# First head of a hybrid streaming step: epsilon rows by a small matmul, queries evacuated sooner, the fourth weight split later on VectorE, values stored ahead of keys

## Chip, cores and metric

One core of a Trainium2 chip runs the whole program in one launch. The metric is the device time in microseconds (us); the median of several executions is compared. Engines are named as the profile does: PE is TensorE, PEld its weight loads, DVE VectorE, ACT ScalarE, POOL GpSimd, SP the queue that issues nearly all DMAs.

## The reference

One layer of an encoder, on 512 frames of a new stream and 64 frames of a running one with 512 cached keys and values. Cut to what matters here:

```python
hn = rmsnorm(x, g_norm1)                       # x / sqrt(mean(x^2) + EPS) * g
proj = hn @ w_in                               # 2048 -> q, k, v (8 heads x 128), gb, gc, hc
q = rmsnorm(q.reshape(B, T, N_HEADS, HEAD_DIM), g_q)
k = rmsnorm(k.reshape(B, T, N_HEADS, HEAD_DIM), g_k)
o_attn = stick_breaking_blocks(q, k_all, v_all, P)   # strictly causal, cached and new keys
...                                            # gated short convolution, output norms
x = x + mix @ w_out
h2 = rmsnorm(x, g_norm2)
x = x + (silu(h2 @ w_gate) * (h2 @ w_up)) @ w_down
# outputs: y, and the new k, v and convolution state of both streams
```

## The kernel before

All 576 tokens (512 + 64) lie along the free axis in two halves of 288, the features on 128 partitions. Every product is made of three passes in a rounded f32 form: each operand is split into a high part (a cast on ScalarE) and a low part (a subtraction, L178 for weights, L225 elsewhere), and TensorE adds high x high, low x high, high x low (`step`, L215). A projection of 128 columns is 2 halves x 16 steps x 3 matmuls. The input norm's row scale isn't applied to x: the projections of q and k use it only through the epsilon of their own norm (EPS times the row's mean square, `eps_r`, 18 columns of 128), and values are multiplied by a broadcast row scale `R1`.

Weights go through a chain: `load_weight` starts a DMA into one of two raw buffers, `split_weight` makes the halves, `next_weight` hands them out in the order q, k, v of head 0, q, k, v of head 1 and so on. So weight 3, the fourth, is the query weight of head 1.

Work other than projections is written as generators on a `Pipeline`. It counts one tick after each step of a projection, 32 to a projection; a generator yields the number of ticks after which it goes on. In head 0 the keys' projection has the ticks 1 to 32, the values' 33 to 64, and head 1's queries begin at 65. The order of TensorE's instructions is this written order throughout, and from head 1 on SP's too. The order of VectorE, ScalarE and GpSimd in the heads (and of SP in head 0) is set by a planner at build time, which simulates all engines and prefers what was written earlier. Each engine then runs its own list strictly in order.

For head 0 the query product is already formed while the input is turned. Then come, as written: the five diagonals `dg` of the row scale, the split of weight 2, and `q_evac` (a 32x32 transpose of the product into `E`, L661, squares L662, sums L663). Behind the keys' projection, `row_scale` makes R1 with five small matmuls (L460), turns it on VectorE (L464) and takes a reciprocal of the square for `eps_r` (L466 to L468). The rest of a norm (`rest`) adds the column sums with one small matmul (ss, L639), makes the reciprocal root (ms L643, y L644 and L645 on ScalarE, t L646 and L647, r L648), scales E (L649), turns it back (qf or kf, L653) and splits it (qh and ql, kh and kl); it runs 38 ticks after the queries' end and 8 after the keys'. For the keys it also makes `kb`, the form that is stored (GpSimd, L651), and starts `attend`.

`attend` begins 24 ticks later in head 0 with the scores z (L708, z0 to z2) and the scores of the cached keys (zs, L734), 10 ticks later stores kb with eight DMAs (L678), after 18 more goes on with the weights (L751 and following) and after 26 more makes the output product po (L772, L775), which needs `vh` and `vl`, the halves of the values. `values` turns the values (L813), stores them to scratch memory 8 ticks after its start, reloads them as `vtok` 12 later (L818, L819), and 8 later stores them to the output (L821, L822) and splits them. `x_sums` forms sums of the input for a later product, in steps between all this. The turned cached keys `kcT` (L831) are made 59 ticks after head 0's start; the buffer of cached keys can be refilled after that.

Of the kernel before, what the change touches and what calls it, by code (L numbers as in the profile page):

```python
# [31 lines left out]
EPS = 1e-6  # L32
# [62 lines left out]
def tile_hybrid_stream_step(  # L95
# [6 lines left out]
    nc = tc.nc  # L102
    mm = nc.tensor.matmul
# [17 lines left out]
    rpad = ctx.enter_context(tc.tile_pool(name="rpad", bufs=1, side="right"))  # L121
    small = rpad.tile([P, 56], F32, name="rpad_t")
    NB = T // 32
    eps_r, gk_t = small[:, :NB], small[:, NB : NB + 32]
    acon = tc.alloc_tile_pool(name="acon", bufs=1, side="left")
    xt_dram = tc.dram_tile([KD, P, T], F32, name="xt_dram")
    x2_dram = tc.dram_tile([KD, P, T], F32, name="x2_dram")
# [33 lines left out]
    ready = []  # L161
# [25 lines left out]
    def split_weight(lo_eng):  # L187
        raw = raws[len(ready)]
        n = specs[len(ready)][1] * specs[len(ready)][2]
        hi, lo = weight_split(len(ready))  # L190
        for a in range(0, n, 1024):
            weight_parts(raw, hi, lo, a, a + 1024, lo_eng)

    pos = [0]

    def next_weight():
        i = pos[0]
        pos[0] += 1
        end = first_out if i < first_out else first_block
        while len(raws) < min(i + 2, end):  # L200
            load_weight()
        while len(ready) < min(i + 2, end):
            split_weight(nc.gpsimd if i == 2 else nc.vector)
        while len(raws) < min(i + 3, end):
            load_weight()
        out = ready[i]
        ready[i] = None
        return out

    pipe = Pipeline()  # L210
# [56 lines left out]
    def misc(name):  # L267
        return ps_z.tile([P, 512], F32, tag="misc", name=name, bufs=2)
# [26 lines left out]

    nhalf = const.tile([P, 5], F32, name="nhalf")
    nc.vector.memset(nhalf, -0.5)

    def col(name, i=0):
        return vec[:, rows[name] + i : rows[name] + i + 1]  # L300
# [150 lines left out]
        nc.gpsimd.tensor_tensor(out=rst, in0=ssr, in1=nhalf, op=ALU.pow)  # L451


    def row_scale():
        psr = misc("ps_r1")
        psr2 = misc("ps_r1s")
        for i in range(5):
            n = P if i < 4 else TS
            dst = psr[:, i * P : (i + 1) * P] if i < 4 else psr2[:, :TS]
            mm(dst, onef[:n, :], dg[:n, i, :n], start=True, stop=True)  # L460
        nc.vector.tensor_copy(R1[:, :TP], psr)
        nc.vector.tensor_copy(R1[:, TP:], psr2[:, :TS])
        turned = tmp.tile([P, T], F32, tag="hl", name="turned")
        nc.vector.transpose(out=turned, in_=R1)  # L464
        first = turned.rearrange("p (b c) -> p b c", c=32)[:, :, 0]
        nc.vector.tensor_tensor(out=eps_r, in0=first, in1=first, op=ALU.mult)  # L466
        nc.vector.reciprocal(out=eps_r, in_=eps_r)
        nc.vector.tensor_scalar(out=eps_r, in0=eps_r, scalar1=EPS, scalar2=None, op0=ALU.mult)  # L468

    hpool.release()  # L470

# [24 lines left out]
        "p (q f t) -> p q f t", q=2, f=2)  # L496
    t1 = tc.alloc_tile_pool(name="t1", bufs=1, reuse_waits="tile", side="left")
    dg = t1.tile([P, 5, P], F32, tag="vtok", name="dg")
    for i in range(5):
        n = P if i < 4 else TS  # L500
        nc.vector.tensor_scalar(out=dg[:n, i, :n], in0=ident[:n, :n], scalar1=rst[:n, i : i + 1], scalar2=None,
                                op0=ALU.mult)
    split_weight(nc.vector)

    def project(evac, banks=(None, None), then=None):
        whi, wlo = next_weight()
# [123 lines left out]
    def norm_evac(name, gcol, dst_f, dst_hi, dst_lo, lag, kb=None, after=None):  # L630
        E = t1.tile([P, T], F32, tag="E", name=f"E{name}", bufs=2)
        Eb = E.rearrange("p (b c) -> p b c", c=32)
        sq = tmp.tile([P, T], F32, tag="hl", name="sq")
        sums = tmp.tile([P, HALF], F32, tag="sq", name="sums")[:, :NB]

        def rest():
            yield lag
            ss = misc("ss")[:, :NB]
            mm(ss, same, sums, start=True, stop=True)  # L639
            ms, t = (tmp.tile([P, HALF], F32, tag=tag, name=tag, bufs=1)[:, :NB] for tag in ("ms", "t"))  # L640
            y, r = (tmp.tile([P, HALF], F32, tag=tag, name=tag)[:, :NB] for tag in ("y", "r"))
            stt = nc.vector.scalar_tensor_tensor
            stt(out=ms, in0=ss, scalar=1.0 / P, in1=eps_r, op0=ALU.mult, op1=ALU.add)  # L643
            nc.scalar.activation(out=y, in_=ms, func=AF.Ln)  # L644
            nc.scalar.activation(out=y, in_=y, func=AF.Exp, scale=-0.5)  # L645
            stt(out=t, in0=y, scalar=-0.5, in1=y, op0=ALU.mult, op1=ALU.mult)  # L646
            nc.vector.tensor_tensor(out=t, in0=t, in1=ms, op=ALU.mult)  # L647
            stt(out=r, in0=t, scalar=1.5, in1=y, op0=ALU.add, op1=ALU.mult)  # L648
            nc.vector.tensor_tensor(out=Eb, in0=Eb, in1=r.unsqueeze(2).to_broadcast([P, NB, 32]), op=ALU.mult)  # L649
            if kb is not None:  # L650
                nc.gpsimd.tensor_tensor(out=kb.rearrange("p (b c) -> p b c", c=32), in0=Eb,  # L651
                                        in1=gk_t.unsqueeze(1).to_broadcast([P, NB, 32]), op=ALU.mult)
            nc.vector.transpose(out=dst_f, in_=E)  # L653
            nc.scalar.activation(out=dst_f, in_=dst_f, func=AF.Copy, scale=gcol)
            e = 3 * P if after else TP
            split(dst_hi[:, :e], dst_lo[:, :e], dst_f[:, :e])
            if after:
                pipe.spawn(after)

        def evac(ps, a, b):  # L660
            nc.vector.transpose(out=E[:, a:b], in_=ps)  # L661
            nc.scalar.activation(out=sq[:, a:b], in_=E[:, a:b], func=AF.Square)  # L662
            nc.vector.reduce_sum(out=sums[:, a // 32 : b // 32], in_=sq[:, a:b].rearrange("p (b c) -> p b c", c=32),  # L663
                                 axis=mybir.AxisListType.X)
            if b == T:
                pipe.spawn(rest())

        return evac
# [6 lines left out]
    def put_tokens(t, dst, a, b):  # L675

        for q in range(4):
            nc.sync.dma_start(out=dst[:, 32 * q : 32 * (q + 1)].rearrange("(b t) c -> t b c", t=32),  # L678
                              in_=t[32 * q : 32 * (q + 1), a:b].rearrange("t (b c) -> t b c", c=32))
# [7 lines left out]
    kw = dict(start=False, skip_group_check=True)  # L687

    def attend(h, st):
        yield 15 + (9 if h == 0 else 0)  # L690
        qf, qh, ql, kf, kh, kl, kcT, cV = (st[n] for n in ("qf", "qh", "ql", "kf", "kh", "kl", "kcT", "cV"))

        z = [ps_z.tile([P, 512], F32, tag=f"z{i}", name=f"z{i}") for i in range(3)]
# [43 lines left out]
        yield 2  # L737
        yield 8
        kb = st["kb"]
        put_tokens(kb, kp[:, h, :], 0, TP)  # L740
        put_tokens(kb, ks[:, h, :], TP, T)

        def weights(b):
            for i in ((2, 3) if b == 2 else (b,)):
# [3 lines left out]
            split(ph[b][:, : width[b]], pl[b][:, : width[b]], pr[b][:, : width[b]])  # L748

        yield 18  # L750
        mm(zb[3], trif, pb[3], stop=False, **kw)  # L751
        mm(zb[2][:, P:], neg1f, pb[3], stop=False, **kw)
        mm(zb[2], trir, ph[2], stop=False, **kw)
# [74 lines left out]
    def keys_cached(st, lag):  # L828
        yield lag
        st["kcT"] = t1.tile([P, TP], F32, tag="kcT", name="kcT")  # L830
        nc.vector.transpose(out=st["kcT"], in_=st["cK"])  # L831

    def head(h):
        st = {}
        st["cK"] = t1.tile([P, TP], F32, tag="cK", name="cK")
        st["cV"] = t1.tile([P, 4, P], F32, tag="cV", name="cV", bufs=2)
        for q in range(4):
            nc.sync.dma_start(out=st["cK"][32 * q : 32 * (q + 1), :].rearrange("t (b c) -> t b c", c=32),
                              in_=ck[:, h, 32 * q : 32 * (q + 1)].rearrange("(b t) c -> t b c", t=32))
        nc.sync.dma_start(out=st["cV"], in_=cv[:, h, :].rearrange("(i p) d -> p i d", p=P))  # L840
        for n in ("q", "k"):
            st[n + "f"] = t1.tile([P, T], F32, tag=n + "f", name=n + "f")
            st[n + "h"] = t1.tile([P, TP], F32R, tag=n + "h", name=n + "h")
            st[n + "l"] = t1.tile([P, TP], F32R, tag=n + "l", name=n + "l")
        st["kb"] = t1.tile([P, T], F32, tag="kb", name="kb")
        q_evac = norm_evac("q", gqs, st["qf"], st["qh"], st["ql"], 13 if h else 38)
        k_evac = norm_evac("k", col("gk"), st["kf"], st["kh"], st["kl"], 16 if h else 8, st["kb"], attend(h, st))
        pipe.spawn(keys_cached(st, 20 if h else 59))
        if h == 0:
            for ps, (a, b) in zip(q0ps, HALVES):  # L850
                q_evac(ps, a, b)
            project(k_evac, (None, "z1"))
            row_scale()
        else:
            project(q_evac)
            project(k_evac)
        Ev = t1.tile([P, T], F32, tag="E", name="Ev", bufs=2)

        def v_evac(ps, a, b):
            nc.vector.tensor_tensor(out=Ev[:, a:b], in0=ps, in1=R1[:, a:b], op=ALU.mult)  # L860

        project(v_evac, ("z2", None) if h == 0 else (None, None))
        pipe.spawn(values(h, st, Ev))
# [1029 lines left out]
```

## Time and profile before

| what | value |
|---|---|
| median of 3 executions | 2367.42 us (2366.43 to 2368.01) |
| the profiled execution's own time | 2369.78 us |
| its span, first to last instruction | 2368.1 us |
| TensorE busy | 2340.6 us, 99% |
| VectorE, ScalarE, GpSimd busy | 80%, 48%, 13% |
| mean granted clock of TensorE | 0.997 |

All times in the trace count from the first instruction. A row of the timeline gives start, duration, engine, line, operation, output and inputs, how many instructions were merged (x2) and, in brackets, how long the engine had been idle and what ended that. A row of the chain of waits has start, duration, engine and line. A row of the waits has the total, the number and the longest. A row of the windows gives the length, then the busy time (and the count) of PE, PEld, DVE, ACT and POOL, then the granted clock of TensorE (1.00 is full speed), the DMA engines' busy share and GB/s.

### The profile page before, as it was taken

The page shows a single profiled execution, that of the slowest core. Times are in us where ns is not written, and L with a number is a line of the kernel's source. Part 1 is how long each engine was busy: PE and PEld are TensorE (multiplying, and loading weights), DVE is VectorE, ACT ScalarE, POOL GpSimd, SP SyncE. Part 2 cuts the span into 40 slices and gives each one's busy share as a digit, 9 for nine tenths or more (in the row PEclk, how much of TensorE's full clock was granted, in tenths as well). Part 3 has the DMA queues.
Part 4 walks back from the last instruction along what each step waited for, and adds up shares of the span by engine and source line. Part 5 has one row for each costly group of instructions (what it writes and reads, how often), then busy time and mean ns, then how long its engine had stood idle before and what let it go on. Part 6 is the DMA issues. An engine that isn't in the chain of part 4 may idle for free.

```text
span 2368.1 us, 43722 instructions
## 1 busy us (share of the span) xinstructions
PE 2340.6 (99%) x17549; PEld 2329.2 (98%) x17549; DVE 1897.4 (80%) x2823; ACT 1134.2 (48%) x1975; POOL 302.3 (13%) x403
## 2 busy tenths in 40 slices
PE   8999999999999999999999999999999999999998
PEld 8899999999999999999999999999999999999998
DVE  8666665788887889888888888888888777987886
ACT  6556555444445555444444444444444444444443
POOL 2111111331111230000000000000000002431222
PEclk9999999999999999999999999999999999999999
DMA  8566554683368654444444444444444935885554
GB/s 259 141 163 167 140 144 117 215 264 118 110 234 220 196 167 140 147 152 131 143 152 127 148 152 128 146 151 128 148 151 131 355 119 200 225 237 198 190 143 86
DMA packets 588996, 395.75 MB, mean 167 GB/s; under 512 B 100222, under 2 KB 577912, under 8 KB 588792
## 3 DMA queue, kind: packets, MB, share of 16 engines
q1 hardware_dynamic: 574968, 375.95, 51.1%
q0 software_dynamic: 8624, 16.22, 3.4%
q8 instruction: 137, 2.24, 0.4%
q10 hardware_dynamic: 5200, 0.79, 0.2%
q14 instruction: 67, 0.55, 0.1%
HBM read 301.46 MB, written 91.44 MB: 166 GB/s over the span
## 4 chain that ended last, share of the span: by engine, by line
PE 88%; DVE 5%; DMA 3%; ACT 2%; issue 1%; ACTq 0%; POOL 0%; SPq 0%; POOLq 0%; DVEq 0%
PE psy L1560 33%; PE psw L1560 16%; PE pj L215 13%; PE psx L1560 8%; PE psy L1064 6%; PE pjo L215 4%; PE psw L1064 3%; PE psx L1064 1%; DVE whl L225 1%; DMA raw_a<-in_w_out_dram 1%; PE z L708 1%; PE po L775 1%; DMA raw_b<-in_w_down_dram 1%; DMA out_dram<-acc 1%; ACT whl L224 0%
## 5 line engine op out<-in xcount | busy, mean ns | idle before, releaser
L1560 PE MATMUL psy<-h_s,whl 128*128 128x288 f32 x2787 | 412.6, 295 | 1.4 <-ACT part L1570 1.4
L215 PE MATMUL pj<-x,whi 128*128 128x288 f32 x1856 | 389.8, 298 | 0.1
L1560 PEld LDWEIGHTS psy<-h_s,whl 128*128 128x128 f32 x2787 | 384.7, 189 | 2.1 <-ACT part L1570 2.1
L225 DVE TENSOR_TENSOR whl<-raw_a,whl 128x1024 fp32r<-128x1024 f32 (+4 forms) x296 | 317.5, 1074 | 54.9 <-ACT whl L224 53.3
L1560 PE MATMUL psw<-t,whl 128*128 128x288 f32 x2400 | 346.8, 294 | 0.0
L1560 PEld LDWEIGHTS psw<-t,whl 128*128 128x128 f32 x2400 | 327.9, 188 | 0.0
L224 ACT CAST whl<-raw_a 128x1024 fp32r<-128x1024 f32 (+4 forms) x296 | 267.6, 906 | 117.0 <-issue 35.4
L215 PEld LDWEIGHTS pj<-x,whi 128*128 128x128 f32 x1856 | 304.9, 190 | 1.1 <-DVE x L366 0.4
L215 PE MATMUL pj<-x,wlo 128*128 128x288 f32 x928 | 275.0, 296 | 0.1
L225 DVE TENSOR_TENSOR whl<-raw_b,whl 128x1024 fp32r<-128x1024 f32 (+5 forms) x190 | 200.9, 1058 | 69.5 <-ACT whl L224 68.6
L224 ACT CAST whl<-raw_b 128x1024 fp32r<-128x1024 f32 (+5 forms) x190 | 164.9, 871 | 169.8 <-issue 73.4
L1570 ACT COPY part<-psy 128x288 f32<-128x288 f32 x242 | 96.3, 398 | 278.6 <-PE psy L1560 257.9
L1560 PE MATMUL psy<-t2t,whl 128*128 128x288 f32 x1212 | 182.9, 294 | 1.1 <-ACT part L1570 1.1
L1560 PE MATMUL psy<-b22m,whl 128*128 128x288 f32 x1212 | 182.8, 294 | 0.0
L215 PEld LDWEIGHTS pj<-x,wlo 128*128 128x128 f32 x928 | 175.4, 189 | 0.7 <-DVE wlo L433 0.3
L1560 PE MATMUL psx<-h_s,whl 128*128 128x288 f32 x1185 | 173.5, 294 | 0.0
L1560 PEld LDWEIGHTS psy<-t2t,whl 128*128 128x128 f32 x1212 | 168.2, 188 | 1.3 <-ACT part L1570 1.3
L1560 PEld LDWEIGHTS psy<-b22m,whl 128*128 128x128 f32 x1212 | 168.0, 188 | 0.3 <-ACT part L1570 0.2
L1560 PEld LDWEIGHTS psx<-h_s,whl 128*128 128x128 f32 x1185 | 162.6, 188 | 0.0
L1339 POOL DMA_DIRECT2D hid_dram<-form x3 | 2.2, 749 | 947.6 <-DVE form L225 947.6
L224 ACT CAST whl<-s 128x1024 fp32r<-128x1024 f32 (+5 forms) x81 | 72.3, 892 | 102.9 <-PE psw L1560 99.4
L1560 PE MATMUL psy<-t,whl 128*128 128x288 f32 x576 | 106.6, 295 | 0.3 <-ACT part L1570 0.3
(472 smaller groups left out, 4308.9 us busy)
## 6 DMA issues: line engine op xcount, KB each, us to landing
hid_dram<-form SPq DMA_DIRECT2D x147, 288.0 KB, 2.3
raw_a<-in_w_in_dram SPq DMA_DIRECT2D x41, 1024.0 KB, 6.1
raw_a<-in_w_gate_dram SPq DMA_DIRECT2D x22, 1024.0 KB, 5.8
raw_a<-in_w_up_dram SPq DMA_DIRECT2D x22, 1024.0 KB, 5.9
raw_b<-in_w_gate_dram SPq DMA_DIRECT2D x22, 1024.0 KB, 6.7
raw_b<-in_w_up_dram SPq DMA_DIRECT2D x22, 1024.0 KB, 6.5
h_s<-hid_dram SPq DMA_DIRECT2D x10, 2016.0 KB, 12.4
raw_a<-in_w_out_dram SPq DMA_DIRECT2D x16, 1024.0 KB, 7.1
```

Of the source, the lines that this page charges most:

```text
L215: mm(ps, w_[:, k, csl], x_, start=(k == 0 and n == 0), stop=(k == nk - 1 and n == 2))
L224: nc.scalar.copy(out=hi, in_=src)
L225: (lo_eng or nc.vector).tensor_tensor(out=lo, in0=src, in1=hi.bitcast(F32), op=ALU.subtract)
L708: mm(zb[i], a_[:, kk], b_[:, q0:TP], start=(n == 0), stop=False, skip_group_check=True)
L775: mm(po[:, i * P : 512], a_[:, i, :], b_[:, : 512 - i * P], stop=(i == 0 and n == 2), **kw)
L1064: mm(ps, whl[:, w_, j, :], x_, start=(start and j == 0 and q == 0), stop=(j == m - 1 and q == 2), skip_group_check=True)
L1339: q.dma_start(out=hid_dram[fp][2 * n - 2 : 2 * n].rearrange("f p t -> p f t"), in_=t.bitcast(F32))
L1560: mm(ps, whl[:, w_, j, :], x_, start=(start and j == 0 and q == 0), stop=(j == len(xs_) - 1 and q == 2), skip_group_check=True)
L1570: nc.scalar.copy(out=t, in_=st["y"])
```

## The change

Everything is in head 0. `eps_r` no longer comes from R1: the row mean squares `ssr` are spread over four quadrant columns (`spread`, a product with the new constant `quad`), and one matmul with `same` (`row_eps`, tick 23) gives the 18 columns, which one VectorE operation scales by EPS. The queries are evacuated ahead of the diagonals and of weight 2's split; R1 (`row_scale`) moves from the end of the keys' projection to tick 29. The rest of the query norm moves from tick 39 to 26, that of the keys from 41 to 39, kcT from 60 to 53, and `attend` from 65 to 67. Weight 3 is split at tick 46 instead of at the start of the values' projection (tick 32), with its subtraction on VectorE instead of GpSimd. The eight stores of kb move 18 ticks back, behind the values' stores.

```diff
@@ next_weight
+    def third_weight():
+        split_weight(nc.vector)
+        yield from ()
...
-        while len(ready) < min(i + 2, end):
-            split_weight(nc.gpsimd if i == 2 else nc.vector)
+        if i == 2:
+            pipe.spawn(third_weight(), 14)
+        while len(ready) < min(i + 2, end) and i != 2:
+            split_weight(nc.vector)
@@ constants
+    nc.vector.memset(quad, 0.0)
+    for j in range(4):
+        nc.vector.memset(quad[32 * j : 32 * (j + 1), j : j + 1], 1.0)
@@ behind the row mean squares
+    spread = tmp.tile([P, HALF], F32, tag="t", name="spread", bufs=1)[:, :20]
+    nc.vector.tensor_tensor(out=spread.rearrange("p (i j) -> p i j", j=4), in0=ssr.unsqueeze(2).to_broadcast([P, 5, 4]),
+                            in1=quad.unsqueeze(1).to_broadcast([P, 5, 4]), op=ALU.mult)
+
+    def row_eps():
+        ps = misc("ps_eps")[:, :NB]
+        mm(ps, same, spread[:, :NB], start=True, stop=True)
+        nc.vector.tensor_scalar(out=eps_r, in0=ps, scalar1=EPS, scalar2=None, op0=ALU.mult)
+        yield from ()
@@ row_scale
-        turned = tmp.tile([P, T], F32, tag="hl", name="turned")
-        nc.vector.transpose(out=turned, in_=R1)
-        first = turned.rearrange("p (b c) -> p b c", c=32)[:, :, 0]
-        nc.vector.tensor_tensor(out=eps_r, in0=first, in1=first, op=ALU.mult)
-        nc.vector.reciprocal(out=eps_r, in_=eps_r)
-        nc.vector.tensor_scalar(out=eps_r, in0=eps_r, scalar1=EPS, scalar2=None, op0=ALU.mult)
+        yield from ()
@@ before the projections
-    for i in range(5):
-        ...
-    split_weight(nc.vector)
+    def row_diagonals():
+        for i in range(5):
+            ...
@@ attend
-        yield 15 + (9 if h == 0 else 0)
+        yield 15 + (13 if h == 0 else 0)
...
-        put_tokens(kb, kp[:, h, :], 0, TP)
-        put_tokens(kb, ks[:, h, :], TP, T)
+        if h:
+            put_tokens(kb, kp[:, h, :], 0, TP)
+            put_tokens(kb, ks[:, h, :], TP, T)
...
         yield 18
+        if not h:
+            put_tokens(kb, kp[:, h, :], 0, TP)
+            put_tokens(kb, ks[:, h, :], TP, T)
@@ head
-        q_evac = norm_evac("q", gqs, st["qf"], st["qh"], st["ql"], 13 if h else 38)
-        k_evac = norm_evac("k", col("gk"), st["kf"], st["kh"], st["kl"], 16 if h else 8, st["kb"], attend(h, st))
-        pipe.spawn(keys_cached(st, 20 if h else 59))
+        q_evac = norm_evac("q", gqs, st["qf"], st["qh"], st["ql"], 13 if h else 25)
+        k_evac = norm_evac("k", col("gk"), st["kf"], st["kh"], st["kl"], 16 if h else 6, st["kb"], attend(h, st))
+        pipe.spawn(keys_cached(st, 20 if h else 52))
         if h == 0:
             for ps, (a, b) in zip(q0ps, HALVES):
                 q_evac(ps, a, b)
+            row_diagonals()
+            split_weight(nc.vector)
+            pipe.spawn(row_eps(), 23)
+            pipe.spawn(row_scale(), 29)
             project(k_evac, (None, "z1"))
-            row_scale()
```

More of the change, by code (lines that the diff above doesn't have):

```diff
@@ L123, in tile_hybrid_stream_step @@
     NB = T // 32
-    eps_r, gk_t = small[:, :NB], small[:, NB : NB + 32]
+    eps_r, gk_t, quad = small[:, :NB], small[:, NB : NB + 32], small[:, NB + 32 : NB + 36]
     acon = tc.alloc_tile_pool(name="acon", bufs=1, side="left")
@@ L498, in tile_hybrid_stream_step @@
     dg = t1.tile([P, 5, P], F32, tag="vtok", name="dg")
-    for i in range(5):
-        n = P if i < 4 else TS
-        nc.vector.tensor_scalar(out=dg[:n, i, :n], in0=ident[:n, :n], scalar1=rst[:n, i : i + 1], scalar2=None,
-                                op0=ALU.mult)
-    split_weight(nc.vector)
+    def row_diagonals():
+        for i in range(5):
+            n = P if i < 4 else TS
+            nc.vector.tensor_scalar(out=dg[:n, i, :n], in0=ident[:n, :n], scalar1=rst[:n, i : i + 1], scalar2=None,
+                                    op0=ALU.mult)
     def project(evac, banks=(None, None), then=None):
```

## The prediction

> **What bounds the kernel now.** I read the page's first part, then who waited for whom on TensorE, then TensorE's order of time around each long wait.
>
> ```profile
> span 2368.1 us, 43722 instructions
> PE 2340.6 (99%) x17549; PEld 2329.2 (98%) x17549; DVE 1897.4 (80%) x2823; ACT 1134.2 (48%) x1975; POOL 302.3 (13%) x403
> PE psx_s L343 <- DMA xsn<-in_x_sample_dram: 5.6, 1, 5.6
> PE z L708 <- ACT kh L224: 2.8, 1, 2.8
> PE po L775 <- ACT vh L224: 2.2, 1, 2.2
> ```
>
> TensorE is busy for 99% of the span, so the end moves only by what TensorE gains or loses. Of its few waits two lie in the first head, the part that the change edits: the scores (z, L708) wait for the key's halves, the output product (po, L775) for the value's halves. Each costs more than its idle time, as the granted clock (last column but two) shows.
>
> ```profile
> 60.00:70.00 10.00, 7.50 (x41) 7.01 (x42) 7.42 (x12) 8.16 (x16) 1.75 (x5) 0.83 0.96 247
> 90.00:100.00 10.00, 7.58 (x32) 6.80 (x32) 3.68 (x7) 3.40 (x6) 1.69 (x5) 0.68 0.01 2
> 494.00:496.00 2.00, 1.45 (x11) 1.22 (x10) 0.96 (x2) 1.16 (x2) 1.49 (x2) 1.00 1.02 317
> 59.25 0.29 PE L215 MATMUL pj<-x,whi 128*128 128x288 f32 x1
> 62.29 0.39 PE L708 MATMUL z<-qh,kh 128*128 128x256 f32 x1 [2.75 <-ACT kh L224]
> 67.49 11.13 PE pj L215 x84
> 117.12 0.35 PE z L708 x3
> 120.03 11.15 PE pj L215 x84
> 91.15 0.38 PE L772 MATMUL po<-pr,vtok 128*128 128x128 f32 x2
> 97.57 8.47 PE pj L215 x54
> 143.75 0.38 PE L772 MATMUL po<-pr,vtok 128*128 128x128 f32 x2
> 145.71 7.17 PE pj L215 x54
> ```
>
> The price of each wait comes from setting head 0 beside head 1, which does the same work without a wait.
> First wait: TensorE stops at 59.54 (59.25 + 0.29) and begins the scores at 62.29: 2.75. From there to the next projection step head 0 takes 67.49 - 62.29 = 5.20, head 1 120.03 - 117.12 = 2.91: 2.29 more. Together 5.04 us.
> Second: from L772 to the next projection step 97.57 - 91.15 = 6.42 against 145.71 - 143.75 = 1.96, so 4.46; then the same 54 matmuls take 8.47 against 7.17, so 1.30. Together 5.76 us. The two are worth 10.8 us, of which 5.0 (2.75 and 2.2) is idling; nearly all of the rest is slow clock afterwards. The stretch 494 to 496, idle for 0.55, keeps the clock at 1.00.
>
> [...]
>
> **First wait, part by part.** Why the keys are late:
>
> ```profile
> 49.17 2.00 ACT L177 CAST whi<-raw_a 128x1024 fp32r<-128x1024 f32 x2 [3.65 <-DMA raw_a<-in_w_in_dram]
> 50.30 4.75 POOL L178 TENSOR_TENSOR wlo<-raw_a,whi 128x1024 fp32r<-128x1024 f32 x2 [10.62 <-ACT whi L177]
> 48.92 0.18 DVE L643 SCALAR_TENSOR_TENSOR ms<-ss,rpad_t 128x18 f32<-128x18 f32 x1 [0.72 <-PE ss L639]
> 51.08 0.21 ACT L644 ACTIVATE y<-ms 128x18 f32<-128x18 f32 x1
> 51.57 1.16 DVE L646 SCALAR_TENSOR_TENSOR t<-y 128x18 f32<-128x18 f32 x1 [2.48 <-ACT y L645]
> 52.76 2.32 DVE L647 TENSOR_TENSOR t<-t,ms 128x18 f32<-128x18 f32 x1
> 56.82 0.14 DVE L647 TENSOR_TENSOR t<-t,ms 128x18 f32<-128x18 f32 x1
> 62.27 0.56 DVE L225 TENSOR_TENSOR kl<-kf,kh 128x384 fp32r<-128x384 f32 x1 [1.38 <-ACT kh L224]
> 109.96 0.18 DVE L643 SCALAR_TENSOR_TENSOR ms<-ss,rpad_t 128x18 f32<-128x18 f32 x1
> 115.09 0.55 DVE L225 TENSOR_TENSOR kl<-kf,kh 128x384 fp32r<-128x384 f32 x1
> 49.60 0.29 PE L639 MATMUL ss<-sums,acA 128*128 128x18 f32 x2
> ```
>
> The queries' ms is there at 49.10, but ScalarE is casting the fourth weight until 51.17, so y comes 2 us late. Then VectorE's two tiny operations take 1.16 and 2.32 while GpSimd splits that weight (50.30 to 55.05); afterwards L647 takes 0.14 on the same shape, and L643, of L646's kind and shape, 0.18. That is 1.0 + 2.2 = 3.2 us lost. Keys queue behind queries on VectorE, so kl ends at 62.83.
>
> Fourth weight: the two casts come at tick 46, not 32, and the subtraction goes to VectorE. Two of its subtractions took 2.36 (next fence). [...]
>
> Queries: their rest moves from tick 39 to 26, keys' from 41 to 39. A tick is 11.13/28 = 0.3975 us, so the keys' column sums leave TensorE near 49.60 - 2 x 0.3975 = 48.8; the queries' sums, at 48.59 before, no longer stand in between, but the new epsilon matmul stands earlier, at about the same price (next fence: 0.26 to 0.29). From ms to the end of kl head 1 needs 115.64 - 109.96 = 5.7. So keys by 48.8 + 0.3 + 5.7 = 54.8; with both casts (2.0) and both subtractions (2.4) wholly in between, 59.2. The scores, moved from tick 65 to 67, are asked for at 59.54 + 0.8 + 0.3 = 60.6. The wait goes, with 1.4 to 5.8 us to spare. TensorE computes at those two ticks, so the later start costs nothing.
>
> **What could be late next in the keys' projection.**
>
> ```profile
> 38.93 2.36 DVE L178 TENSOR_TENSOR wlo<-raw_a,whi 128x1024 fp32r<-128x1024 f32 x2 [0.54 <-ACT whi L177]
> 41.21 1.02 DVE L501 TENSOR_SCALAR dg<-ident,rst 128x128 f32<-128x128 f32 x5
> 42.16 0.83 DVE L661 STREAM_TRANSPOSE Eq<-pj 128x288 f32<-128x288 f32 x2
> 43.29 1.12 DVE L663 TENSOR_REDUCE sums<-sq 128x9 f32<-128x288 f32 x3
> 44.36 1.05 PE L460 MATMUL ps_r<-dg,acA 128*128 128x128 f32 x8
> 48.59 0.29 PE L639 MATMUL ss<-sums,acA 128*128 128x18 f32 x2
> ```
>
> That projection ends at 44.36, so its ticks 23, 26 and 29 lie at 40.8, 42.0 and 43.2. VectorE there has the query transposes ahead of the diagonals (1.02) and the split (2.36) instead of behind: transposes from 38.6 to 39.4, then at worst one of the two subtractions (1.18) while ScalarE squares, then two sums (0.75): 41.4, in time for 42.0. Its whole bundle (spread 0.2, 0.83, three sums 1.12, 1.02, 2.36) is 5.5 from 38.4, ending at 43.9; the epsilon copy and ms may come last, near 44.2, and the R1 matmuls of 43.2 need the PSUM buffers that these two free. A wait of 0 to 1.5; I take 0.5, because the second subtraction and the keys' sum are not asked for before the values' projection, and the planner can set them behind. Below 0.55 the clock holds, as seen at 494. TensorE's added work is one small matmul, 0.29 by the L639 row. Removing the turn, reciprocal and copy relieves VectorE by some 1.4, off the path. The five new memsets of quad fall in the start, where TensorE waits 5.6 for samples: nothing.
>
> **Second wait.**
>
> ```profile
> 93.19 0.51 ACT L224 CAST vh<-vtok 128x384 fp32r<-128x384 f32 x1
> 139.29 0.51 ACT L224 CAST vh<-vtok 128x384 fp32r<-128x384 f32 x1
> 68.59 4.55 SPq L678 DMA_DIRECT2D out_dram<-kb  x8
> 73.25 0.39 SPq L818 DMA_DIRECT2D vtok<-vt_dram  x1
> 76.25 0.38 SPq L821 DMA_DIRECT2D out_dram<-vtok  x1
> 124.98 0.38 SPq L818 DMA_DIRECT2D vtok<-vt_dram  x1
> ```
>
> The values are back by 76.25, since their store starts, yet ScalarE casts them at 93.19: it is the planned order, not the data. Head 1 casts 4.46 ahead of L772 (143.75), head 0 2.04 behind. What differs ahead of it is the reload: 10.96 after the scores' start in head 0 (73.25 - 62.29), 7.86 in head 1 (124.98 - 117.12). The change takes the eight key stores, 4.55 of SP's time, out from in front: 6.4, earlier than head 1's. So the planner should place the cast where head 1 has it, or sooner. The key stores now stand ahead of the sixth and later weight loads, but behind the same value stores; the sum of SP's work there is unchanged, and those weights are split some 30 ticks later. I cost that at nothing; without that cover it is at most the 4.55.
>
> **Sum.** -5.0 - 5.8 + 0.3 + 0.5 = -10.0 us. All later heads follow TensorE, so nothing gives it back. The profiled execution took 2369.78 (1.7 outside its span) and would take 2359.8; it lies 2.4 above the median, so 2357.4.
>
> **The rivals.**
> A, the vh cast keeps its late place: only the first wait goes, -5.0 + 0.8 = -4.2, 2363.2. For it: the order is planned, which I can't see. Against: head 1's place. Chance 0.13.
> B, the planner keeps the query transposes behind the split: sums at 44.4, asked for at 42.0; 2.4 of idling is as long as the gaps that slowed the clock, with 2.3 more as behind the first: -10.5 + 4.7, 2361.6. Against: the new order of emission. 0.10.
> C, the keys' cast and subtraction of the fourth weight keep the first wait alive, only the second goes: -5.8 + 0.8, 2362.4; 0.05, as it needs over 1.4 beyond the worst sum.
> D, slower: heads 1 to 7 repeat one order, and kl there ends at 115.64 for scores at 117.12, 1.5 us of margin. VectorE does the x_sums products between; with SP's queue changed the planner may put one more of these blocks ahead of kl. A wait of 2.5 with its slow clock is 5 us a head, 35 in seven: 2392. It decides from the third head on. Against: nothing is edited there. 0.10.
>
> **Numbers.** The forecast has 0.62, and with unknown costs of -1 to +1.5 downstream spans 2355 to 2360. The range, 2354 to 2365, also takes in A, B and C and leaves out D and a few hundredths. About 0.2% (4.7 us) is what a measurement can tell: below 2362.7 lie the forecast and parts of A, B and C, 0.76; within, the rest of them, 0.14; above 2372.2, D, 0.10.
>
> **What would show it.** Right: no TensorE wait at L708 or L775, clock 1.00 from 60 to 110, L647 near 0.14, vh ahead of L772. Wrong: a wait at L639 or L460 in 40 to 46, vh still behind qh, or waits of 2 us and more in later heads.

## The result, and the profile after

| kernel | median | lowest to highest, executions |
|---|---|---|
| before | 2366.06 us | 2364.29 to 2369.39, 9 |
| after | 2360.80 us | 2359.23 to 2366.10, 9 |

The ratio is 0.998 [0.9972, 0.9989], that is 5.3 us less, with 2.6 to 6.6 us as the interval. The forecast was 10.0 us less, 2357.4, counted from 2367.42, the median of before's first three executions; 2360.8 lies inside its range.

The profiled execution of after took 2360.45 us. These are its span and the line of who waited for whom on TensorE that counts.

```profile
span 2358.7 us, 43730 instructions
PE ss L654 <- DVE sums L678: 2.5, 2, 1.7
```

The two waits of the first head, at the scores (L708 before, L723 now) and at the output product (L775, now L794), are gone from the list. A new one is there, second only to the wait for samples at the start: the small matmul that adds the column sums (L639 before, L654 now) waits for VectorE's sums (L663, now L678), twice, 2.5 us in all. Lines have shifted: the queries' and keys' transpose is L676 now, the casts and subtractions of halves L230 and L231, the tiny norm operations L658 to L663, the step of a projection L221, po L791 and L794, the reload of the values L837.

After's windows and its timeline, where before had its two waits:

```profile
60.00:70.00 10.00, 10.00 (x76) 9.87 (x76) 6.20 (x10) 7.19 (x15) 2.17 (x5) 1.00 0.68 195
90.00:100.00 10.00, 10.00 (x75) 9.86 (x74) 5.46 (x8) 5.88 (x9) 0.49 (x2) 1.00 0.00 1
57.16 0.56 DVE L231 TENSOR_TENSOR kl<-kf,kh 128x384 fp32r<-128x384 f32 x1 [0.65 <-ACT kh L230]
63.39 0.28 PE L723 MATMUL z<-qh,kh 128*128 128x256 f32 x1
73.96 0.50 ACT L230 CAST vh<-vtok 128x384 fp32r<-128x384 f32 x1
90.33 0.22 PE po L791 x2
66.46 11.15 PE pj L221 x84
92.14 7.17 PE pj L221 x54
```

TensorE is busy for all of 60 to 70 and of 90 to 100 at the full clock; before it was busy 7.50 and 7.58 at 0.83 and 0.68. The keys are split at 57.72 for scores that begin at 63.39, so 5.7 us to spare. The values' cast stands 16.4 us ahead of its product instead of 2.04 behind. From the scores to the next projection step it is 3.07 (before 5.20), from po to the next one 1.81 (before 6.42), and the 54 matmuls take 7.17 again.

The new wait, again from after's timeline:

```profile
38.89 2.36 DVE L178 TENSOR_TENSOR wlo<-raw_a,whi 128x1024 fp32r<-128x1024 f32 x2 [0.33 <-DMA xt_dram<-o_ob]
41.26 0.84 DVE L676 STREAM_TRANSPOSE Eq<-pj 128x288 f32<-128x288 f32 x2
43.11 0.40 PE L654 MATMUL ss<-sums,acA 128*128 128x18 f32 x2 [0.80 <-DVE sums L678]
49.13 1.05 ACT L177 CAST whi<-raw_a 128x1024 fp32r<-128x1024 f32 x1 [0.40 <-DMA raw_a<-in_w_in_dram]
50.09 0.44 ACT L677 ACTIVATE sq<-Ek 128x288 f32<-128x288 f32 x1
50.22 1.23 DVE L178 TENSOR_TENSOR wlo<-raw_a,whi 128x1024 fp32r<-128x1024 f32 x1 [0.76 <-ACT whi L177]
51.36 0.45 DVE L678 TENSOR_REDUCE sums<-sq 128x9 f32<-128x288 f32 x1
51.96 0.37 PE L654 MATMUL ss<-sums,acA 128*128 128x18 f32 x2 [1.72 <-DVE sums L678]
52.32 3.70 PE pjz L221 x27
53.77 0.18 DVE L662 TENSOR_TENSOR t<-t,ms 128x18 f32<-128x18 f32 x1
```

Queries: the planner still put their transposes (41.26) behind weight 2's subtractions (38.89), and TensorE waits 0.80. Keys: their squares on ScalarE (50.09) stand behind the fourth weight's first cast (49.13), which itself waits for that weight's DMA, and their last sum on VectorE (51.36) behind the first subtraction (50.22). But for that cast ScalarE is free from 48.74, where qh's ends, so by this order the cast holds the squares back by 1.35 and the subtraction the sum by another 0.83 (50.53 to 51.36). TensorE asks two ticks earlier than before and waits 1.72; the 27 matmuls behind the wait take 3.70. Further down, L662 takes 0.18, not 2.32.

### The profile page after: what moved, and what is told of

Read it like the earlier page. It is cut to its first block, busy times and chain, and to the rows that moved or that the text cites. A ratio compares the mean times of both kernels' runs of the same rounds, so it can differ in the third digit from the quotient of the medians.

```text
span 2358.7 us, 43730 instructions
## 1 busy us (share of the span) xinstructions
PE 2335.9 (99%) x17551; PEld 2325.3 (99%) x17551; DVE 1894.6 (80%) x2828; ACT 1134.9 (48%) x1975; POOL 300.3 (13%) x401
## 4 chain that ended last, share of the span: by engine, by line
PE 89%; DVE 5%; DMA 3%; issue 1%; ACT 1%; SPq 0%; POOL 0%; ACTq 0%; POOLq 0%; DVEq 0%
PE psy L1582 34%; PE psw L1582 17%; PE pj L221 13%; PE psx L1582 8%; PE psy L1086 6%; PE pjo L221 4%; PE psw L1086 3%; PE psx L1086 1%; DMA raw_a<-in_w_out_dram 1%; DVE whl L231 1%; PE po L794 1%; PE z L723 1%; DVE whl L1058 1%; DMA out_dram<-acc 0%; DVE x L375 0%
## 5 line engine op out<-in xcount | busy, mean ns | idle before, releaser
L221 PE MATMUL pj<-x,whi 128*128 128x288 f32 x1856 | 388.6, 298 | 0.2
L231 DVE TENSOR_TENSOR whl<-raw_a,whl 128x1024 fp32r<-128x1024 f32 (+4 forms) x296 | 318.2, 1076 | 54.6 <-ACT whl L230 53.1
L230 ACT CAST whl<-raw_a 128x1024 fp32r<-128x1024 f32 (+4 forms) x296 | 267.5, 906 | 113.1 <-issue 35.4
L221 PEld LDWEIGHTS pj<-x,whi 128*128 128x128 f32 x1856 | 303.6, 189 | 1.4 <-DVE x L375 0.7
L221 PE MATMUL pj<-x,wlo 128*128 128x288 f32 x928 | 274.3, 296 | 0.1
L231 DVE TENSOR_TENSOR whl<-raw_b,whl 128x1024 fp32r<-128x1024 f32 (+5 forms) x190 | 200.2, 1054 | 69.5 <-ACT whl L230 68.2
L230 ACT CAST whl<-raw_b 128x1024 fp32r<-128x1024 f32 (+5 forms) x190 | 164.9, 871 | 170.3 <-issue 73.5
L221 PEld LDWEIGHTS pj<-x,wlo 128*128 128x128 f32 x928 | 174.7, 188 | 0.7 <-DVE wlo L442 0.3
L230 ACT CAST whl<-s 128x1024 fp32r<-128x1024 f32 (+5 forms) x81 | 72.2, 892 | 102.8 <-PE psw L1582 99.4
```

What stands on the lines that cost most here:

```text
L221: mm(ps, w_[:, k, csl], x_, start=(k == 0 and n == 0), stop=(k == nk - 1 and n == 2))
L230: nc.scalar.copy(out=hi, in_=src)
L231: (lo_eng or nc.vector).tensor_tensor(out=lo, in0=src, in1=hi.bitcast(F32), op=ALU.subtract)
```

## The experiments

All profiles are cut at the same five points, since the executions shown differ by up to 2.9 us at the start (the first input DMAs) and by 3.5 us behind pjo. Start is the first matmul of the second half of the keys' projection, z0 and z1 are the scores of heads 0 and 1, po head 0's output product, pjo the first output projection. The first row is before's profile, then a second one of the same kernel; the last two columns are the median and its ratio to before in the same series. In us:

| kernel | start | to z0 | to po | to z1 | start to z1 | z1 to pjo | pjo to end | median | ratio |
|---|---|---|---|---|---|---|---|---|---|
| before | 38.01 | 24.28 | 28.86 | 25.81 | 78.95 | 664.87 | 1586.27 | 2366.06 | |
| before_again | 39.77 | 24.00 | 28.87 | 24.63 | 77.50 | 665.03 | 1584.70 | 2367.35 | 0.9998 [0.9989, 1.0007] |
| stores_alone | 39.56 | 23.36 | 27.33 | 20.06 | 70.75 | 664.32 | 1584.17 | 2362.76 | 0.9978 [0.9968, 0.9988] |
| weight_alone | 38.56 | 22.73 | 29.72 | 20.34 | 72.79 | 664.37 | 1586.08 | 2363.50 | 0.9980 [0.9971, 0.9989] |
| after | 37.97 | 25.42 | 26.78 | 19.24 | 71.44 | 664.25 | 1585.04 | 2360.80 | 0.9980 [0.9972, 0.9989] |
| after_again | 38.11 | 26.77 | 26.78 | 19.24 | 72.79 | 664.89 | 1584.11 | 2361.38 | 0.9974 [0.9965, 0.9984] |
| gpsimd_again | 39.56 | 24.52 | 26.78 | 19.24 | 70.54 | 665.96 | 1585.14 | 2360.46 | 0.9971 [0.9960, 0.9983] |
| keys_stored_first | 40.84 | 24.89 | 26.78 | 19.24 | 70.91 | 664.29 | 1583.96 | 2363.05 | 0.9980 [0.9971, 0.9989] |
| queries_three_ticks_later | 39.02 | 26.77 | 26.78 | 19.24 | 72.79 | 664.34 | 1585.55 | 2363.39 | 0.9984 [0.9975, 0.9993] |
| keys_ahead_of_weight | 38.51 | 23.37 | 26.78 | 19.24 | 69.39 | 666.10 | 1584.40 | 2361.55 | 0.9976 [0.9968, 0.9985] |
| key_sums_asked_later | 38.24 | 23.37 | 26.78 | 19.25 | 69.40 | 665.15 | 1583.71 | 2360.23 | 0.9964 [0.9952, 0.9977] |
| both_sums_asked_later | 39.74 | 22.49 | 26.79 | 19.24 | 68.52 | 664.82 | 1582.82 | 2358.54 | 0.9961 [0.9948, 0.9975] |
| stores_and_later_scores | 39.15 | 23.75 | 27.11 | 17.62 | 68.48 | 664.28 | 1585.59 | 2360.10 | 0.9966 [0.9954, 0.9979] |

The columns to z0 and to z1 depend on where a kernel places its scores; start to z1 is the sum to compare. For the same reason a time in one profile is set beside one in another only as its distance from start. My theory at the outset was the prediction's: late key stores set the values free, and the slow L647 together with ScalarE's cast made the keys late. ("Slow L647" stands for what the prediction's rows show: L647 takes 2.32 us beside GpSimd's subtraction and 0.14 after it.) The rivals were that one part does both, that moving the subtraction to VectorE is not needed, and, for the missing gain, that the new wait at L654 comes from the weight's split standing ahead of the sums.

**before_again** (no edit)

> The kernel before, unchanged, to see how much its own two waits cost in another execution. Theory 1: the two waits and the slow clock behind them cost 10.8 us in every execution, so the profile shows about 5.0 and 5.8 again, and the gain of 5.3 at the median was reduced by new waits alone. Theory 2: the length of the slow clock is a matter of the moment, so the profile first shown had it long; then here the stretch at half clock behind one of the waits is shorter by over a microsecond or missing, and the two cost 6 to 9 us together. Time: within 0.1% of before.

```profile
63.77 0.38 PE L708 MATMUL z<-qh,kh 128*128 128x256 f32 x1 [2.42 <-ACT kh L224]
69.00 11.11 PE pj L215 x84
92.64 0.38 PE L772 MATMUL po<-pr,vtok 128*128 128x128 f32 x2
99.06 7.27 PE pj L215 x54
```

Worked out as in the prediction, against the same rows of head 1: first wait 2.42 + (5.23 - 2.91) = 4.74, second 6.42 - 1.96 = 4.46 and 0.10 for the 54 matmuls, 9.3 us in all. In the first profile it was 10.8. The first wait repeats to 0.3; what differs more is how much slow clock follows (the 54 matmuls lose 0.10 here, 1.30 there).

**stores_alone**: before, and of the change only the later key stores.

```diff
-        put_tokens(kb, ...)
+        if h:
+            put_tokens(kb, ...)
...
         yield 18
+        if not h:
+            put_tokens(kb, ...)
```

> The kernel before with one part of the change: the eight key stores of the first head 18 ticks later, behind the value stores. Theory 1 (the stores in front set where the planner puts the cast of the values): the cast of vh comes ahead of L772, no TensorE wait at the output product, the wait for kh stays at about 2.8: -5.8 us in a profile, -3 to -6 at the median. Rival (the place of the cast is set by the late values of the first head, not by the stores): vh still behind qh or less than 1 us earlier, the wait for vh stays above 1.5, time within 1 us of before.

```profile
62.92 0.39 PE L708 MATMUL z<-qh,kh 128*128 128x256 f32 x1 [1.83 <-ACT kh L224]
66.58 11.15 PE pj L215 x84
85.34 0.53 ACT L224 CAST vh<-vtok 128x384 fp32r<-128x384 f32 x1
90.25 0.38 PE L776 MATMUL po<-pr,vtok 128*128 128x128 f32 x2
```

The values' cast comes 4.9 us ahead of the output product, and that wait is gone. The first stays at 1.83, costs 1.83 + (3.66 - 2.91) = 2.6 us, and the clock behind it stays at 1.00 (60 to 70). This one move of eight DMAs gave 4.6 us (2362.76 against 2367.39).

**weight_alone**: before, and of the change only the fourth weight's later split on VectorE.

```diff
-        while len(ready) < min(i + 2, end):
-            split_weight(nc.gpsimd if i == 2 else nc.vector)
+        if i == 2:
+            pipe.spawn(third_weight(), 14)
+        while len(ready) < min(i + 2, end) and i != 2:
+            split_weight(nc.vector)
```

> The kernel before with one part of the change: the fourth weight split at tick 46 with its subtraction on VectorE. Theory 1 (the 3.2 us that two tiny VectorE operations lose beside GpSimd are what makes the keys late): L646 and L647 take under 0.2, kl ends about 3 us earlier and the wait at the scores falls from 2.8 to under 0.5: -3 to -5 us. Rival (VectorE's own list is what counts: its two subtractions now stand ahead of the norm's operations and wait for the cast): the tiny operations are fast, but kl ends within 1 us of before, the wait stays between 2 and 4, time within 1.5 us of before.

```profile
PE z L714 <- ACT kh L230: 1.1, 1, 1.1
PE z L714 <- DVE kl L231: 1.0, 1, 1.0
51.18 1.22 DVE L178 TENSOR_TENSOR wlo<-raw_a,whi 128x1024 fp32r<-128x1024 f32 x1
52.89 0.18 DVE L649 SCALAR_TENSOR_TENSOR ms<-ss,rpad_t 128x18 f32<-128x18 f32 x1
53.82 0.18 DVE L653 TENSOR_TENSOR t<-t,ms 128x18 f32<-128x18 f32 x1
62.08 0.55 DVE L231 TENSOR_TENSOR kl<-kf,kh 128x384 fp32r<-128x384 f32 x1
64.00:66.00 2.00, 2.00 (x9) 1.80 (x8) 0.56 (x1) 2.00 (x5) 0.06 (x1) 0.50 1.14 323
89.30 0.50 ACT L230 CAST vh<-vtok 128x384 fp32r<-128x384 f32 x1
91.01 0.38 PE L778 MATMUL po<-pr,vtok 128*128 128x128 f32 x2
```

Two surprises. The slow L647 is gone (L653, the old L647, takes 0.18 where it took 2.32), yet kl ends 24.07 us behind the start (62.63 - 38.56) where it was 24.82 in before (62.83 - 38.01), 0.75 earlier and not 3: the split's two subtractions now stand on VectorE ahead of the queries' ms (14.33 behind the start, in before 10.91). Most of what the slow L647 cost, VectorE's own work costs again; a wait of 2.2 and half clock (0.50 in 64 to 66) remain. And the second wait goes although the key stores keep their place: the planner moved the values' cast ahead of L778. So the late stores are enough for that, but not the only thing that is, and the median gains 3.9 us although the first wait stays.

**after_again** (no edit to after)

> The kernel after, unchanged, beside the variants below and with a second profile. Theory (new waits of 2.5 us and a changing price of the old ones explain the gap between 10 us forecast and 5.3 measured): the two waits for the sums (L654) appear again, 2 to 3 us together, no wait at the scores or the output product, no slow clock before 110 us; 2360 to 2363, 4 to 7 us below before. Rival (the waits for the sums were a matter of that one execution): under 1 us here.

```profile
51.94 0.37 PE L654 MATMUL ss<-sums,acA 128*128 128x18 f32 x2 [1.59 <-DVE sums L678]
52.31 5.19 PE pjz L221 x27
52.00:54.00 2.00, 2.00 (x11) 2.00 (x12) 1.93 (x6) 0.44 (x2) 0.00 (x0) 0.67 1.04 314
54.00:56.00 2.00, 2.00 (x10) 2.00 (x10) 1.69 (x3) 0.20 (x1) 0.92 (x1) 0.50 0.46 78
56.00:58.00 2.00, 2.00 (x16) 2.00 (x16) 0.46 (x2) 1.08 (x2) 0.29 (x1) 0.97 0.50 73
```

The new wait repeats (2.3 us in all), and this time, unlike what was expected, the clock falls behind it: the 27 matmuls that took 3.70 in after's profile take 5.19 here. So the new wait costs 2.5 in one execution and 2.3 + 1.5 = 3.8 in another.

**gpsimd_again**: after, with the fourth weight's subtraction back on GpSimd, still late.

```diff
     def third_weight():
-        split_weight(nc.vector)
+        split_weight(nc.gpsimd)
```

> The kernel after with the fourth weight's subtraction back on GpSimd, still at tick 46. In the kernel after TensorE waits 0.8 us for the queries' sums and 1.7 for the keys' sums, because the keys' last sum stands behind one cast (ScalarE) and one subtraction (VectorE) of that weight. Theory 1 (VectorE's share of that wait is about half): the keys' wait falls to 0.6 to 1.0; the tiny operations that run beside GpSimd take 1 to 2.4 again, but the scores have the slack and show no wait; 0.5 to 1 us faster than the kernel after. Rival (moving the subtraction to VectorE was needed for the scores): kl ends after the scores are asked for, a wait of over 1 us returns at the scores with slow clock, 2 to 5 us slower than the kernel after.

```profile
52.67 0.37 PE L654 MATMUL ss<-sums,acA 128*128 128x18 f32 x2 [0.90 <-DVE sums L678]
54.22 2.32 DVE L662 TENSOR_TENSOR t<-t,ms 128x18 f32<-128x18 f32 x1
59.75 0.56 DVE L231 TENSOR_TENSOR kl<-kf,kh 128x384 fp32r<-128x384 f32 x1 [1.05 <-ACT kh L230]
64.08 0.28 PE L723 MATMUL z<-qh,kh 128*128 128x256 f32 x1
```

The slow L647, now L662, is back (2.32), kl ends 20.75 us behind the start (19.75 in after, 20.36 in after_again), and nobody waits for it: the scores begin 3.8 us after kl. Start to z1 is 70.54 against 71.44, because the keys' wait is 0.90 instead of 1.72. That the rest of the wait is ScalarE's cast is read from the order in after's timeline; no run moves the cast alone. Moving the subtraction to VectorE was not needed for the gain; by this profile it made about half of the new wait.

**keys_stored_first**: after, with the key stores back in their old place.

```diff
-        if h:
-            put_tokens(kb, ...)
+        put_tokens(kb, ...)
...
-        if not h:
-            put_tokens(kb, ...)
```

> The kernel after with the eight key stores back in their old place, ahead of the value stores. Theory 1 (the cast of the values is late because the first head's values are late, and any of the parts that brings them forward is enough, as the weight alone did): vh stays ahead of L791, no wait at the output product, time within 1 us of the kernel after. Rival (the stores must be out of the way): vh falls behind qh or L791, a wait of 1 to 2.5 us with slow clock returns, 2 to 6 us slower than the kernel after.

```profile
68.17 4.52 SPq L693 DMA_DIRECT2D out_dram<-kb  x8
72.79 0.39 SPq L833 DMA_DIRECT2D vtok<-vt_dram  x1
87.59 0.51 ACT L230 CAST vh<-vtok 128x384 fp32r<-128x384 f32 x1
92.51 0.38 PE L787 MATMUL po<-pr,vtok 128*128 128x128 f32 x2
```

The stores are in front of the reload again, and the cast still comes 4.9 us ahead of L787, without a wait. Start to z1 (70.91) is no worse than in after; the medians (2363.05 and 2361.38) have overlapping intervals. With the rest of the change in place the moved stores bring nothing that these runs can tell.

**queries_three_ticks_later**: after, with the queries' sums asked for at tick 29 instead of 26.

```diff
-        q_evac = norm_evac("q", ..., 13 if h else 25)
+        q_evac = norm_evac("q", ..., 13 if h else 28)
-            pipe.spawn(row_scale(), 29)
+            pipe.spawn(row_scale(), 31)
```

> The kernel after with the rest of the query norm at tick 29 instead of 26 and R1 at 31 instead of 29. Theory (the queries' sums are ready at 43.06, and the column sums are asked for 0.8 us too early): the first of the two waits for sums goes, the second stays at 1.2 to 2: 0.5 to 1 us faster in a profile, not to be told from noise in the time. Rival (the later queries push the keys): the second wait grows by as much as the first falls, or a wait at the scores returns.

```profile
52.80 0.37 PE L654 MATMUL ss<-sums,acA 128*128 128x18 f32 x2 [2.50 <-DVE sums L678]
53.17 5.21 PE pjz L221 x27
```

The queries' wait is gone, the keys' grows from 1.72 to 2.50 and brings the slow clock (0.58 and 0.56 in the windows from 54 to 58, 5.21 for the 27 matmuls against 3.70 in after): nothing won. TensorE comes to the keys' sums earlier by what it didn't wait before, and they are not ready any sooner.

**keys_ahead_of_weight**: the same, and during the values' projection of head 0 VectorE and ScalarE keep the written order, in which the weight comes after the keys.

```diff
-        project(v_evac, ("z2", None) if h == 0 else (None, None))
+        with ExitStack() as first:
+            if h == 0:
+                first.enter_context(tc.manual_schedule(engines={mybir.EngineType.Activation, mybir.EngineType.DVE}))
+            project(v_evac, ("z2", None) if h == 0 else (None, None))
```

> As the one before, and VectorE and ScalarE take the instructions of the values' projection of head 0 in the written order instead of the planned one, so that the keys' last sum and their whole norm stand ahead of the fourth weight's casts and subtractions. Theory (the keys' sums wait for that weight in both engines' lists): both waits for sums are gone (under 0.3 together), the weight is ready by about 58, before head 1's queries at 59 to 60, no wait at the scores: 2.5 us faster than the kernel after, about 2358. Rival (the fourth weight then comes too late, or the keys' sums wait for something else): a wait of 1 us and more at head 1's first projection steps, or still at the sums, and no gain.

```profile
50.47 0.37 PE L654 MATMUL ss<-sums,acA 128*128 128x18 f32 x2 [0.69 <-DVE sums L678]
56.14 2.36 DVE L178 TENSOR_TENSOR wlo<-raw_a,whi 128x1024 fp32r<-128x1024 f32 x2 [0.40 <-ACT whi L177]
```

With the subtractions behind the keys, the keys' wait falls from 2.50 to 0.69 in the same series: the split in front of the sums made most of it. (The written order holds for the whole of the values' projection, so this run does not part the cast from the subtraction.) Start to z1 gains 3.4 us on queries_three_ticks_later; 1.8 of it is missing again between z1 and pjo (666.10 against 664.34): TensorE's wait for ScalarE's `part` (L1089) is 1.9 there against 0.6, and head 1's output product waits 0.3 for vl. Why is not shown. The median gains 1.8; the waits of under 0.3 and the 2358 that were expected did not come.

**key_sums_asked_later** and **both_sums_asked_later**: after, with the order left to the planner and the matmuls of the sums asked for later; the scores keep their place.

```diff
@@ key_sums_asked_later
-        yield 15 + (13 if h == 0 else 0)
+        yield 15 + (8 if h == 0 else 0)
-        k_evac = norm_evac("k", ..., 16 if h else 6, ...)
+        k_evac = norm_evac("k", ..., 16 if h else 11, ...)
@@ both_sums_asked_later: lag 13 and 6 in these lines instead of 11 and 8, and
-        q_evac = norm_evac("q", ..., 13 if h else 25)
+        q_evac = norm_evac("q", ..., 13 if h else 28)
-            pipe.spawn(row_scale(), 29)
+            pipe.spawn(row_scale(), 31)
```

> The kernel after with the keys' rest at tick 44 instead of 39, and attend's own delay shorter by as much, so that the scores are still asked for at tick 67. Theory (the new wait is only a matter of asking too early: the keys' sums are ready at 51.8, and kl has over 5 us of slack before the scores): the wait of 1.6 to 1.7 for the keys' sums and any slow clock behind it are gone, the queries' 0.8 stays, no wait at the scores; from the second half of the keys' projection to head 1's scores 69.5 to 70.2 us, against 71.4 and 72.8 in the two profiles of the kernel after; 1.5 to 3 us faster. Rival (the planner lets everything behind slip by the same amount): the wait stays over 1 us or comes back at the scores.

> The kernel after with the queries' rest at tick 29, R1 at 31, the keys' rest at 46 and the scores still at 67. Theory as before, for both waits: no wait of 0.5 us or more in head 0, clock 1.00 throughout, 68.7 to 69.5 us from the second half of the keys' projection to head 1's scores, 2.5 to 4 us faster than the kernel after if the later stages stay as they are. Rival (as with the queries alone three ticks later, the keys' sums come later still): a wait of over 1 us for the keys' sums with slow clock, no gain.

The windows of both_sums_asked_later:

```profile
40.00:60.00 20.00, 20.00 (x153) 19.73 (x152) 15.62 (x37) 7.81 (x15) 2.44 (x2) 1.00 0.82 241
60.00:80.00 20.00, 20.00 (x153) 19.86 (x152) 14.42 (x26) 13.50 (x29) 2.84 (x6) 1.00 0.62 163
```

In key_sums_asked_later the keys' wait is gone and the queries', 0.8, is left; here, between 40 and 80, TensorE has no gap at all and the full clock. Start to z1 is 68.52, 10.4 less than before's profile and 9.0 less than before_again's. 2358.54 us is the lowest median of all kernels, 0.9961 of before, [0.9948, 0.9975], where after stands at 0.998 and 0.9974 in its two series; with five executions its interval overlaps theirs, as it does those of key_sums_asked_later and of the next kernel.

**stores_and_later_scores**: stores_alone, and the scores asked for six ticks later.

```diff
-        yield 15 + (9 if h == 0 else 0)
+        yield 15 + (15 if h == 0 else 0)
```

> The kernel before with two small parts only: the key stores behind the value stores, and the scores six ticks (2.4 us) later. The epsilon rows, the queries and the fourth weight stay as before. Theory (the first wait is a matter of when TensorE is sent to the scores, and the projections can fill that time): no wait at the output product, the wait for kh falls from 1.8 to 2.7 to under 0.5 and no slow clock: about 68.5 to 69.5 us from the second half of the keys' projection to head 1's scores, 1 to 3 us faster than the kernel after. Rival (a later start of the scores pushes all of the first head's chain and shows again at the output product or in head 1): a wait of over 1 us there, or the stage is no shorter than 70.7, that of the stores alone.

```profile
62.07 0.51 ACT L224 CAST kh<-kf 128x384 fp32r<-128x384 f32 x1
62.90 0.28 PE L708 MATMUL z<-qh,kh 128*128 128x256 f32 x1
```

The keys are as late as ever (kl ends 24.0 us behind the start, 23.9 in stores_alone), with the fourth weight's split and cast in their old place, and no one waits: TensorE fills the six ticks with projection steps. The margin is thin, as the scores begin 0.3 us after kh. Start to z1 is 68.48, the same as with all the other parts and the retimed sums; the median, 2360.10, can't be told from after's. In these runs two moved pieces do what the whole change does.

## Why the prediction was right and wrong

**Right: both waits go, and nothing later gives it back.** The keys end at 57.72, inside the 54.8 to 59.2 worked out; the clock is 1.00 from 60 to 70 and from 90 to 100; L647's successor takes 0.18; heads 1 to 7 carry no new wait (z1 to pjo 664.25 and 664.89 against 664.87 and 665.03), so rival D did not come, and neither did A or C. With the new wait removed as well the stage gains 10.4 and 9.0 us, which is the price of the two waits, 10.8 and 9.3, less about 0.3 for the new matmul.

**The step that failed: the waits for the column sums.** The prediction's term, "A wait of 0 to 1.5; I take 0.5", stands for the keys' projection, 40 to 46. There the queries' sums waited 0.80 and 0.76, inside that range and one of the signs of being wrong that the prediction names; it is rival B's order with a smaller price, transposes behind weight 2's split, 0.8 at full clock instead of the 2.4 and slow clock given there. The larger wait, for the keys' sums in the values' projection, has no term in the sum: 1.72 in one profile, 1.59 with 1.5 of slow clock in the other. It was in a sentence that I passed over: the keys' sums were moved two ticks up, and the fourth weight into their neighbourhood, written at tick 46. I took the written tick for a lower bound on where the planner puts the work; it put the cast and the first subtraction ahead of the keys' squares and last sum, and keys_ahead_of_weight shows that this order makes most of the wait (2.50 to 0.69). I checked the keys against the scores, 5.7 us off, and not against the matmul of their own sums, which TensorE meets first.

**The price of the waits was one execution's.** 10.8 in the profile shown, 9.3 in the next. The length of the waits repeats to 0.3, the slow clock behind them doesn't (1.30 and 0.10 lost by the 54 matmuls in before's two profiles, 0 and 1.5 by the 27 in after's). And the gap of 0.55 at 494, which the prediction takes as what the clock bears, is only the front of one of 1.48 that ends at 496.93 (psx, L1064); the windows from 494 to 498 have the clock at 1.00 all the same.

**The last step, "it lies 2.4 above the median, so 2357.4", carried over an excess.** After's profiled execution took 2360.45, its median is 2360.80. The profile forecast for it was 2359.8, and 0.65 us off; the median was 3.4 off. Before's profiled execution was itself a dear one, 3.7 above the median of its nine, and no such excess is found in after's. Its stages say where the 9.4 us between the spans (2368.1 and 2358.7) lie: 7.5 from start to z1, 0.6 from z1 to pjo, 1.2 behind it; the last two stand in code that isn't edited. So that the profile came so close is luck: the edited stage gave 7.5 of the 10.0, and unedited stages happened to give 1.8. In the second pair, before_again and after_again, the edited stage gives 77.50 - 72.79 = 4.7, beside medians that differ by 5.3 and 5.8. From the rows it should be -9.3 + 0.3 + 2.3 + 1.5 = -5.2. How the median's 5.3 divides between waits, slow clock and the variable ends stays open, with one profile for each kernel.

**Reasons that were not the ones.** The slow L647 (2.32) on VectorE and the cast on ScalarE do delay the keys, but the split on VectorE delays them nearly as much (weight_alone, kl 24.07 behind the start against 24.82), and gpsimd_again has the slow L647 and loses nothing. In after kl ends 19.75 behind the start, 5.1 earlier than in before, and with the slow L647 back (gpsimd_again, 20.75) it is still 4.1 earlier. That is what the earlier queries with their epsilon, the keys' two ticks and the weight's later place do together; no run parts them, and the weight's place with its subtraction on VectorE gave 0.75 alone. The scores' two later ticks, 0.8 us, were not needed for it. Later scores do as well: six ticks remove that wait where the stores have moved too (stores_and_later_scores), and without the stores they were not run. The late key stores remove the second wait when they are the only edit; in after they could stay (keys_stored_first). There are two ways to the same placement of the cast, and the prediction knew one.

## What to carry to other kernels

Where the critical engine has filling work, the cheapest cure for a wait is to ask later: here moving a consumer by six ticks did as much as making its producer 5 us faster. Of every step that is moved up, look first at the next thing that the critical engine asks of it, not at the last one, and don't read the written place of a neighbour as its place in a planned order. The price of a wait that costs clock should come from two or three executions, and no fixed offset joins a profile to a median.

## What the runs showed of the hardware

After some waits TensorE's granted clock is 0.50 for a stretch. In after_again's three windows it is 0.33 x 2 / 0.5 = 1.3, 2.0 and 0.1 us, 3.4 in all, which by that count is worth 1.7 us of full speed; the 27 matmuls lost 1.5. In before, by windows of 0.1 us, it lasts from 62.87 to 66.28 behind the first wait, 3.4 us, and from 93.59, 0.16 before the end of the second, to 100.42, 6.8 us (96 to 98 has 0.50 too):

```profile
94.00:96.00 2.00, 1.80 (x6) 1.50 (x7) 0.48 (x2) 0.00 (x0) 0.00 (x0) 0.50 0.04 8
98.00:100.00 2.00, 2.00 (x10) 2.00 (x9) 0.70 (x1) 0.84 (x2) 0.00 (x0) 0.50 0.00 0
```

In before_again the stretch behind the second wait is 3.4 us (0.93, 0.50 and 0.72 in the windows from 94 to 100), which makes most of the difference between 10.8 and 9.3.

Whether it sets in does not follow from the length of the gap alone: 1.72 (after) and 1.83 (stores_alone) left the clock at 1.00, 1.59 (after_again) did not, nor did the waits of 2.2 and more in head 0 (2.75 and 2.22 in before, 2.42 and 2.22 in before_again, 2.50 in queries_three_ticks_later). The plainest pair is one later wait, at the sums of the second norm (L500): TensorE is busy for 8.46 of 880 to 890 in after and in after_again. The wait is 1.37 long in after (until 883.35), and behind it the clock is 0.67, 0.50 and 0.97 in the windows from 884 to 890; in after_again, where it is 1.4 and TensorE idles for 1.50 of 884 to 886, the clock is 1.00 from 884 to 894. In before the same sums (L486) wait 1.46, until 891.61, and the clock is 0.50 from 892.31 to 895.72; in before_again they wait 1.9 between 890 and 894, and the clock is 1.00 there. What decides is not shown.
